# Layer 0's second MLP product half by seven quarter products, with the remainder dealt out under the first attention

## The chip, the cores and the metric

The kernel runs on one core of one Trainium2 chip. The metric is the device time of one launch in microseconds (us); lower is better. The engines are named as in the profile: PE is the matrix engine, PEld its weight load, DVE the vector engine, ACT the scalar engine, POOL the general engine, SP the engine that issues nearly all DMAs.

## What is computed

Two decoder layers on 1024 tokens of width 1024, in float32. Layer 0 mixes with a gated convolution of 31 taps and an attention on 256 memory rows; layer 1 with a three-branch sparse attention (compressed, selected, window) and a memory attention. Behind each mixing stand an output projection and an MLP:

```python
x = x + mix @ w_out[l]
x = x + squared_relu_mlp(rms_norm(x, norm_mlp_g[l]), w_mlp_in[l], w_mlp_out[l])

def squared_relu_mlp(h, w_in, w_out):          # w_in 1024 x 4096, w_out 4096 x 1024
    return jnp.square(jax.nn.relu(h @ w_in)) @ w_out
```

Layer 1's mixing reads `x` as it stands behind layer 0's MLP, so all of that MLP for a token's half must be done before the half's attention is prepared.

## The kernel before

**Halves and tiles.** The tokens are two halves of 512 (`hf` 0 and 1). Activations lie with the width on the partitions, as 8 tiles of 128x512 (`x[hf][o]`, `act[kt]`). Every float32 product is made of three matmuls: an operand is split into a high part (ACT copies it to the matmul type, L90 or L113) and a low part (the difference, L91 or L114, on DVE or POOL), and high-high, high-low and low-high are summed in a PSUM bank. `mm3` (L83 to L85) issues such triples. One 128x512 matmul is the unit in which work is counted below.

**Order of the work.** Half 0 goes through layer 0 first: mixing, output projection (`w_out`, L413 to L415, tile `ps_wo`), MLP. Under half 0's MLP run half 1's projections and its convolution (`conv`, L715), each of whose six channel tiles is released by a mark, a pair of instructions in half 0's MLP named by the list `MB`. Then come half 1's `w_out`, the preparation of half 0's attention (norm and projections; tiles `ps_kc`, `ps_tok`), and that attention with half 1's layer-0 MLP beside it; after that half 0's output projection of layer 1, the preparation of half 1's attention, and that attention with half 0's layer-1 MLP dealt out under it; last half 1's `w_out` and the remaining products of layer 1's MLP. The order on each engine is set when the program is built, by a list scheduler that fills an engine's gaps from what is ready, by priority of program order; `issue_after` bars an instruction from being placed ahead of another. A `Feed` deals a generator of steps out between the attention's transposes: at each mark it takes steps until the done share equals the share of the attention that has passed.

**Layer 0's MLP** is `mlp`. For each of 16 chunks of 256 hidden rows, `proj_in` makes two hidden tiles (48 matmuls into `ps_i`, L454 to L456; the ReLU times the norm's factor on DVE at L465, square on ACT at L466, split at L90 and L91 into `hid`) and `proj_out` adds their products to the eight `x` tiles (48 matmuls into `ps_mo`, the add on DVE at L479). 768 matmuls a half go into each of the two products. `HELD` = 2 chunks' `proj_out` of half 0 come behind half 1's `w_out`, with whose norm (`inv_rms`) they share the time. The sum of squares for the next norm is taken tile by tile behind the last chunk (`after0`); `norm_steps` then sums it over the partitions (`ps_n`, L154), takes the root on DVE (L99, L100) and spreads the factor (`ps_r`, L168); DVE multiplies it into `h` (L182).

**Layer 1's MLP** has its second product by seven products of quarters instead of eight (class `Seven`). A chunk's two hidden tiles by two halves of the tokens are one 2x2 matrix of blocks, its weights another. P1 and P2 are plain and use half 0 alone (`outs`; P1 is gathered in the tiles `p1`, and added to both halves on POOL by `add_p1`, L688). For the others `late` fetches half 0's hidden tiles from memory (`hd`), makes half 1's (`pairs`, `hidden`, L522 to L524 and L528), forms sums and differences (four on DVE, `te`, and four on POOL, `sv`, L653 to L660), splits them, and multiplies: the chain P6, P7, P4 and the chain P5, P3 each leave a running sum in one PSUM bank (L679), which after each product is added to other tiles of `x` (L681).

## Time and profile before

| | |
|---|---|
| three runs | 2396.56, 2399.91, 2400.14 us; median 2399.91 us |
| the profiled execution | 2395.2 us, of which the span of the profile is 2393.4 us |
| busy over the span | PE 2313.6 us, PEld 1963.5, DVE 1733.0, POOL 1394.2, ACT 1301.2 |
| mean granted clock of PE | 0.985 of full speed |
| DMA | 259.25 MB, on average 108 GB/s |

The profiled execution is 1.4 us below the fastest of the three runs and 4.7 us below their median. Stages in the profile, by the tiles that PE writes: up to 252 us layer 0's mixing; 252 to 303 half 0's `w_out`; 303 to 651 half 0's MLP with the convolution of half 1; 651 to 732 half 1's `w_out` and what was held back; 732 to 897 the preparation of attention 0; 897 to 1204 attention 0; 1204 to 1290 the rest of half 1's MLP; 1290 to 1461 half 0's `w_out` of layer 1 and the preparation of attention 1; 1461 to 1932 attention 1; 1932 to 2035 half 1's `w_out` and the entry into the quarter products; 2035 to 2393 these products. In a row of windows a busy time is followed by the number of instructions, PEclk is the granted clock, and the last two columns are the mean busy share of the DMA engines and GB/s.

### The profile page before, as it was taken

The numbers are of one execution on the slowest core, as the hardware profiler recorded it, in microseconds if no ns is written. First come the engines' busy times: TensorE is split into PE (matmuls) and PEld (weight loads), VectorE is DVE, ScalarE is ACT, GpSimd is POOL, SyncE is SP. The second block draws the span as 40 slices with busy tenths as digits, with TensorE's granted clock in tenths as the row PEclk, the third lists the DMA queues.
The fourth block names the chain that finished last, engine by engine and source line by source line (L and its number), as shares of the span: only waits on it lengthen the run. The fifth ranks groups of instructions, "written<-read, shape, count | busy, mean of one in ns | idle before, by whom it ended". The sixth has DMA issues, their size and how long they took to land.

```text
span 2393.4 us, 36549 instructions
## 1 busy us (share of the span) xinstructions
PE 2313.6 (97%) x11926; PEld 1963.5 (82%) x11926; DVE 1733.0 (72%) x3476; ACT 1301.2 (54%) x2974; POOL 1394.2 (58%) x1280
## 2 busy tenths in 40 slices
PE   6998899999999899999999999999999999999999
PEld 5887687888778798888887888788888877888887
DVE  7897577998646857677654865777778856777777
ACT  5575555333544446777644555777777743333332
POOL 5866544455653325756645224476676628878975
PEclk8999899999999999999999999899999999999999
DMA  5212433323343424222235543322222245332331
GB/s 190 83 55 80 153 102 99 101 99 97 116 151 104 150 85 127 83 90 79 82 118 173 151 137 105 125 72 76 92 80 78 81 143 193 119 107 93 110 97 58
DMA packets 161823, 259.25 MB, mean 108 GB/s; under 512 B 18145, under 2 KB 49505, under 8 KB 161121
## 3 DMA queue, kind: packets, MB, share of 16 engines
q1 hardware_dynamic: 161632, 256.91, 33.4%
q8 instruction: 95, 1.56, 0.3%
q14 instruction: 96, 0.78, 0.1%
HBM read 217.52 MB, written 28.84 MB: 103 GB/s over the span
## 4 chain that ended last, share of the span: by engine, by line
PE 84%; DVE 6%; DMA 3%; issue 3%; ACT 2%; POOL 1%; SPq 0%; ACTq 0%; POOLq 0%; DVEq 0%
PE ps_mo L679 9%; PE ps_mo L83 5%; PE ps_mo L84 5%; PE ps_mo L85 5%; PE ps_i L455 4%; PE ps_i L456 4%; PE ps_i L454 4%; PE ps_i L522 4%; PE ps_i L524 4%; PE ps_i L523 4%; PE ps_t L1269 4%; PE ps_s L1226 4%; PE ps_o L1287 2%; PE ps_wo L413 2%; PE ps_wo L414 2%
## 5 line engine op out<-in xcount | busy, mean ns | idle before, releaser
L114 POOL TENSOR_TENSOR hl<-raw,hl 128x512 fp32r<-128x512 f32 x504 | 665.0, 1330 | 569.4 <-ACT hl L113 529.2
L113 ACT ACTIVATE hl<-raw 128x512 fp32r<-128x512 f32 x552 | 344.0, 629 | 463.0 <-PE ps_i L456 121.5
L679 PE MATMUL ps_mo<-leaf,wl 128*128 128x512 f32 x960 | 225.9, 389 | 0.3 <-DVE leaf L91 0.3
L522 PE MATMUL ps_i<-act,hl 128*128 128x512 f32 x512 | 210.9, 412 | 4.8 <-DVE b L528 4.1
L83 PE MATMUL ps_mo<-hid,hl 128*128 128x512 f32 x512 | 205.5, 402 | 9.8 <-DVE a L465 4.4
L679 PEld LDWEIGHTS ps_mo<-leaf,wl 128*128 128x128 f32 x960 | 180.2, 188 | 38.0 <-DVE leaf L91 0.7
L454 PE MATMUL ps_i<-act,hl 128*128 128x512 f32 x512 | 200.9, 392 | 3.1 <-ACT r L433 3.1
L524 PE MATMUL ps_i<-act,hl 128*128 128x512 f32 x512 | 201.2, 393 | 0.4 <-POOL hl L114 0.4
L455 PE MATMUL ps_i<-act,hl 128*128 128x512 f32 x512 | 201.5, 394 | 0.0
L456 PE MATMUL ps_i<-act,hl 128*128 128x512 f32 x512 | 201.3, 393 | 0.0
L85 PE MATMUL ps_mo<-hid,hl 128*128 128x512 f32 x512 | 201.1, 393 | 0.0
L84 PE MATMUL ps_mo<-hid,hl 128*128 128x512 f32 x512 | 201.1, 393 | 0.0
L523 PE MATMUL ps_i<-act,hl 128*128 128x512 f32 x512 | 200.8, 392 | 0.0
L479 DVE TENSOR_TENSOR x<-x,ps_mo 128x512 f32<-128x512 f32 x256 | 173.5, 683 | 33.1 <-PE ps_mo L85 31.7
L1279 DVE TENSOR_TENSOR PT<-ps_t,PT 128x512 fp32r<-128x512 f32 (+1 forms) x220 | 147.8, 673 | 48.3 <-ACT PT L1275 46.1
L1255 POOL TENSOR_TENSOR prob<-prob,small 128x1024 f32<-128x1024 f32 (+3 forms) x120 | 181.9, 1532 | 0.0
L1275 ACT ACTIVATE PT<-ps_t 128x512 fp32r<-128x512 f32 (+1 forms) x256 | 143.8, 566 | 59.9 <-PE ps_t L1269 57.6
L1238 ACT ACTIVATE prob<-ps_s,small 128x512 f32<-128x512 f32 (+3 forms) x240 | 141.5, 591 | 61.3 <-DVE small L1236 48.3
L1226 PE MATMUL ps_s<-KS,Q 128*128 128x512 f32 (+5 forms) x552 | 144.5, 361 | 3.8 <-ACT prob L1238 3.8
L681 DVE TENSOR_TENSOR x<-x,ps_mo 128x512 f32<-128x512 f32 x160 | 106.5, 681 | 41.5 <-PE ps_mo L679 40.9
L715 DVE SCALAR_TENSOR_TENSOR ca<-vB,taps,ca 128x512 f32<-128x512 f32 x174 | 130.6, 751 | 2.1
L83 PEld LDWEIGHTS ps_mo<-hid,hl 128*128 128x128 f32 x512 | 96.7, 189 | 33.5 <-DVE x L479 7.8
(341 smaller groups left out, 6268.8 us busy)
## 6 DMA issues: line engine op xcount, KB each, us to landing
raw<-in_w_mlp_in_dram SPq DMA_DIRECT2D x256, 256.0 KB, 2.7
raw<-in_w_mlp_out_dram SPq DMA_DIRECT2D x160, 256.0 KB, 2.8
...
```

The costliest lines, as they stand in the source:

```text
L83: nc.tensor.matmul(ps, lhsT=lh, rhs=rh, start=(i == 0), stop=False)
L84: nc.tensor.matmul(ps, lhsT=lh, rhs=rl, start=False, stop=False)
L85: nc.tensor.matmul(ps, lhsT=ll, rhs=rh, start=False, stop=(i == n - 1))
L113: nc.scalar.activation(hl[:, 0, :n], raw[:, :n], AF.Copy)
L114: k.last_lo = k.lo_eng.tensor_tensor(hl[:, 1, :n], raw[:, :n], hl[:, 0, :n].bitcast(F32), op=ALU.subtract)
L454: nc.tensor.matmul(p_, lhsT=wh, rhs=h[kt][:, 0], start=kt == 0, stop=False)
L455: nc.tensor.matmul(p_, lhsT=wh, rhs=h[kt][:, 1], start=False, stop=False)
L456: nc.tensor.matmul(p_, lhsT=wl, rhs=h[kt][:, 0], start=False, stop=kt == KT - 1)
L522: nc.tensor.matmul(ps, lhsT=wh, rhs=h[kt][:, 0], start=kt == 0, stop=False)
L523: nc.tensor.matmul(ps, lhsT=wh, rhs=h[kt][:, 1], start=False, stop=False)
L524: nc.tensor.matmul(ps, lhsT=wl, rhs=h[kt][:, 0], start=False, stop=kt == KT - 1)
L679: nc.tensor.matmul(ps[i], lhsT=ws[y][:, u, m], rhs=bs[y][:, v], start=z + y + q == 0, stop=y == self.G - 1 and q == 2, skip_group_check=z > 0)
```

## The change

The plain `mlp` goes; layer 0 too is run by `Seven`, with chunks 0 to 7 plain (`whole`) and chunks 8 to 15 `cut`. Half 0 makes all its hidden tiles, the plain outputs, and of the cut chunks P1 and P2; `HELDM` = 96 of these matmuls stand behind half 1's `w_out`. Then `lates` runs half 1's hidden tiles of the cut chunks with P6, P7 and P4, on the PSUM banks `s` (three) and `ca`, and stores two weight sums and two hidden differences a chunk in memory (`sd`). P5 and P3 (`fifth`) read them back: together with half 1's plain chunks and with part of layer 1's output projection of half 0 (`w_part`, five of eight input tiles, whose sum goes through memory as `xq`) they are dealt out by a `Feed`, `AHEAD0` = 380 matmuls before attention 0's first transposes and the rest under it. Half 0's `w_out` of layer 1 keeps three input tiles, 72 matmuls instead of 192. The norm and first projections of attention 1 use the banks and pools of the work beside it (`km`), which lets them be placed under the end of attention 0. The low parts of weights in layer 0's `lates` go to DVE, POOL, POOL in turn (`Turns`).

```diff
+MIXORDP = (0, 1, 2, 6, 7, 3, 4, 5)
-MQB, HELD = 2, 2
+MQB = 2
 HOP, MEMHOP, AHEAD = 1, 3, 192
-MB = (1, 3, 4, 6, 8, 9)
+MB = (4,8,11,14,17,20)
+PLAIN, HELDM, AHEAD0, END0 = 8, 96, 380, 1.0
...
-def w_out(k, l, mix, x, resid, order):
+def w_out(k, l, mix, x, resid, order, runs=None):
...
+    runs = runs or (order[:4], order[4:])
...
-        for g, kts in ((order[0] // 4, order[:4]), (order[4] // 4, order[4:])):
-            w = [weights(k, k.i["w_out"][l, o + i][:, 512 * g:512 * g + 512], P) for i in range(WG)]
+        for kts in runs:
+            lo, n = min(kts), len(kts)
+            w = [weights(k, k.i["w_out"][l, o + i][:, P * lo:P * (lo + n)], P) for i in range(WG)]
...
+def w_part(k, l, mixd, leaf, runs, resid, dst):
...
+    for o in range(KT):
+        t = k.tmp.tile([P, HF], F32, tag="a", name="t", bufs=2)
+        nc.sync.dma_start(t, resid[:, o])
+        ps = k.psum.tile([P, HF], F32, tag=k.tag, name="ps_wo", bufs=k.nps)
+        for kts in runs:
+            w = weights(k, k.i["w_out"][l, o][:, P * kts[0]:P * (kts[-1] + 1)], P)
+            for kt in kts:
+                wh, wl = (w[kt - kts[0]][:, x] for x in range(2))
+                nc.tensor.matmul(ps, lhsT=wh, rhs=mix[kt][:, 0], start=kt == runs[0][0], stop=False)
+                nc.tensor.matmul(ps, lhsT=wh, rhs=mix[kt][:, 1], start=False, stop=False)
+                nc.tensor.matmul(ps, lhsT=wl, rhs=mix[kt][:, 0], start=False, stop=kt == runs[-1][-1])
+                if kt == runs[-1][-1]:
+                    nc.vector.tensor_add(t, t, ps)
+                    nc.sync.dma_start(dst[:, o], t)
+                yield 3
...
-def mlp(k, l, x, act, rms, after, order, held=0):
...
+class Turns:
+
+
+    def __init__(self, *engines):
+        self.engines, self.n = engines, 0
+
+    def tensor_tensor(self, *args, **kw):
+        self.n += 1
+        return self.engines[self.n % len(self.engines)].tensor_tensor(*args, **kw)
...
-    if not r:
+    if not r and lead:
...
+        if not (r or lead or g):
+            next(rms)
...
-            ps = [psum.tile([P, HF], F32, tag="mm", name="ps_mo", bufs=6) for _ in range(4)]
+            ps = [psum.tile([P, HF], F32, tag=t, name="ps_mo", bufs=n) for t, n in BANKS[self.l]]
...
+    def fifth(self, cs, kept):
+
+        k, nc, x = self.k, self.k.nc, self.x
+        ws, hs = ([], []), ([], [])
+        for z in range(2):
+            for c in cs:
+                ws[z].append(weight(k, kept(c)[z]))
+                raw = k.wpool.tile([P, 512], F32, tag="raw", name="raw", bufs=k.nraw)
+                nc.sync.dma_start(raw, kept(c)[2 + z])
+                hs[z].append(self.leaf())
+                split(nc, hs[z][-1][:, 0], hs[z][-1][:, 1], raw)
+        for two in ((0, 1), (2, 3)):
+            ps = [k.psum.tile([P, HF], F32, tag=k.tag, name="ps_mo", bufs=k.nps) for _ in two]
+            for z in range(2):
+                for i, p_ in zip(two, ps):
+                    m = slice(i * P, i * P + P)
+                    for y in range(self.G):
+                        w, h = ws[z][y], hs[z][y]
+                        for q, (u, v) in enumerate(((0, 0), (0, 1), (1, 0))):
+                            nc.tensor.matmul(p_, lhsT=w[:, u, m], rhs=h[:, v], start=z + y + q == 0,
+                                             stop=y == self.G - 1 and q == 2, skip_group_check=z > 0)
+                    o = (4, 0)[z] + i
+                    nc.vector.tensor_add(x[1][o], x[1][o], p_)
+                    k.pe(3 * self.G * HF / 2.4)
+                    yield 3 * self.G
+
+    def lates(self, pool, psum, groups, rms, chains, after, sizes, kept=None, sums=None):
...
             self.late(pool, psum, cs, cur, chains, after if last else None, sizes, kept)
-            if 0 < g < 5:
-                self.add_p1(g - 1)
+            for hf, i in (sums or PSUMS)[g]:
+                self.add_p1(i, hf)
             cur = nxt
 
+BANKS = ((('s', 3),) * 3 + (('ca', 1),), (('mm', 6),) * 4)
+PSUMS = [[]] + [[((0, 1), i)] for i in range(4)] + [[]] * 3
 CHAINS = (((6, 1, 0), (7, 1, 4), (4, 0, 4)), ((5, 1, 4), (3, 1, 0)))
...
-        with tc.tile_pool(name=f"na{hf}", bufs=1, side="right") as k.tmp:
-            k.start(norm_steps(k, h, x, [acc], None))
-            k.flush()
+        if hf:
+            km.start(norm_steps(km, h, x, [acc], None, k.lo_eng))
+            km.flush()
+        else:
+            with tc.tile_pool(name=f"na{hf}", bufs=1, side="right") as k.tmp:
+                k.start(norm_steps(k, h, x, [acc], None))
+                k.flush()
...
-        acc = []
-        rest0 = mlp(k, 0, x[0], act[0], r, after0(0, acc), MIXORD0, HELD)
-        marks = next(rest0)
+        more = pool(es, "hid2")
+        acc, acc1 = [], []
+        hd0, sd, hd = (dram.tile([16, n, P, HF], F32, name=nm) for n, nm in ((2, "hd0"), (4, "sd"), (2, "hd")))
+        groups = [(c, c + 1) for c in range(0, 16, 2)]
+        whole, cut = groups[:PLAIN // 2], groups[PLAIN // 2:]
+
+        def kept(c):
+            return [sd[c, j] for j in range(4)]
+
+        GORD = cut + whole
+        p1p = [ExitStack() for _ in range(2)]
+        p1 = [pool(p1p[i // 2], f"p1{i}").tile([P, HF], F32, name=f"p1{i}") for i in range(4)]
+        m0 = Seven(k, 0, x, act, (MIXORD0, MIXORD), p1, more, pslot[0], hd0, range(PLAIN, 16))
+        todo = Feed(k, m0.plain(GORD, 0, r), 0, 1)
+        todo.take(48 * 16 + 24 * PLAIN + 24 * 16 - HELDM)
         k.flush()
...
         for i in range(6):
-            with tc.issue_after(marks[MB[i]][0].ins), tc.issue_after(marks[MB[i]][1].ins):
+            with tc.issue_after(m0.marks[MB[i]][0].ins), tc.issue_after(m0.marks[MB[i]][1].ins):
                 conv(k, i, vB[i], taps, cvs[i], csum, None, NDVEB)
...
                 r = iter(list(w_out(kl, 0, act[1], x[1], ins["x"][1], MIXORD)))
-        list(rest0)
+        list(todo.steps)
+
+        def after(p, i):
+            if p in (6, 4):
+                after0(0, acc)({6: i, 4: 4 + i}[p])
+
+        with tc.tile_pool(name="st0", bufs=1, side="right") as st:
+            n = len(cut)
+            k.lo_eng = Turns(nc.vector, nc.gpsimd, nc.gpsimd)
+            m0.lates(st, k.psum, cut, r, CHAINS[:1], after, {"b1": 6, "wr": 8, "ws": 3, "bt": 3}, kept,
+                     [[]] + [[((0, 1)[:1 + i // 2], i) for i in range(4) if i * (n - 2) // 4 + 1 == g] for g in range(1, n)])
+            k.flush()
+        k.lo_eng = nc.gpsimd
         psA.close()
         k.psum = es.enter_context(psum_pool("ps2"))
         k.nps = 2
+        p1p[1].close()
 
...
-        attend(0, acc[0], lambda: None)
-        acc = []
-        list(mlp(k, 0, x[1], act[1], r, after0(1, acc), MIXORD))
+        act[0] = act_tiles(0)
+
+        def rest_of_h1():
+            for i, cs in enumerate(cut):
+                yield from m0.fifth(cs, kept)
+                if i in (1, 2):
+                    m0.add_p1(i - 1, (1,))
+            yield from m0.plain(whole, 1, None, after0(1, acc1))
+
+        xq = dram.tile([P, KT, HF], F32, name="xq")
+        n = 24 * len(cut) * 2 + 96 * PLAIN + 120
+        feed = []
+
+        def part():
+            assert feed[0].at > 8 * MEMHOP + 42 * HOP
+            yield from w_part(k, 1, mixd[0], m0.leaf, ((6, 7), (0, 1, 2)), xs[0], xq)
+
+        def between():
+            todo = (y for s in (rest_of_h1, part) for y in s())
+            feed.append(Feed(k, todo, n, (8 * MEMHOP + 84 * HOP) * END0))
+            feed[0].take(AHEAD0)
+            feed[0].total, feed[0].done = n - feed[0].done, 0
+            return feed[0]
+
+        attend(0, acc[0], between)
+        list(feed[0].steps)
         k.flush()
-        hd = dram.tile([16, 2, P, HF], F32, name="hd")
-        groups = [(c, c + 1) for c in range(0, 16, 2)]
-        m1 = Seven(k, 1, x, act, (MIXORD, MIXORD1), None, pool(es, "hid2"), pslot[0], hd, range(16))
+        p1p[0].close()
+        m1 = Seven(k, 1, x, act, (MIXORDP, MIXORD1), None, more, pslot[0], hd, range(16))
...
             act[0], x[0] = act_tiles(0), x_tiles(0)
-            load_mix(k, act[0], mixd[0], MIXORD, k.wpool, "raw", k.nraw)
-            rms0 = w_out(k, 1, act[0], x[0], xs[0], MIXORD)
+            load_mix(k, act[0], mixd[0], (3, 4, 5), k.wpool, "raw", k.nraw)
+            rms0 = w_out(k, 1, act[0], x[0], xq, MIXORDP, ((3, 4, 5),))
...
-        attend(1, acc[0], between)
+        attend(1, acc1[0], between)
```

By the built programs, 128x512 matmuls of the MLPs' second products are 2784 where they were 2880; those of the hidden tiles and output projections are as many as before.

DVE at the norm of attention 0 (`h` is the normed tile, `act` its low part or a tile of it, `x_5771` and the like an `x` tile of half 1), before:

```order
L182 TENSOR_TENSOR h<-ps_r,x_2552 128x512 x2
L465 SCALAR_TENSOR_TENSOR a<-ps_i,r 128x512
L91 TENSOR_TENSOR act_94<-h,act_94 128x512
L479 TENSOR_TENSOR x_5771<-x_5771,ps_mo 128x512
L91 TENSOR_TENSOR act_95<-h,act_95 128x512
L182 TENSOR_TENSOR h<-ps_r,x_2553 128x512
L91 TENSOR_TENSOR hid<-a,hid 128x512
L479 TENSOR_TENSOR x_5771<-x_5771,ps_mo 128x512
L182 TENSOR_TENSOR h<-ps_r,x_2553 128x512
L91 TENSOR_TENSOR act_96<-h,act_96 128x512
L479 TENSOR_TENSOR x_5772<-x_5772,ps_mo 128x512
L182 TENSOR_TENSOR h<-ps_r,x_2554 128x512
```

and after, where `leaf<-raw` is the low part of what `fifth` has read back, and L700 its add into `x`:

```order
L700 TENSOR_TENSOR x_5426<-x_5426,ps_mo 128x512
L184 TENSOR_TENSOR h<-ps_r,x_2552 128x512 x2
L700 TENSOR_TENSOR x_5426<-x_5426,ps_mo 128x512
L93 TENSOR_TENSOR act_7651<-h,act_7651 128x512
L700 TENSOR_TENSOR x_5427<-x_5427,ps_mo 128x512
L93 TENSOR_TENSOR act_7652<-h,act_7652 128x512
L184 TENSOR_TENSOR h<-ps_r,x_2553 128x512
L93 TENSOR_TENSOR leaf<-raw,leaf 128x512
L184 TENSOR_TENSOR h<-ps_r,x_2553 128x512
L700 TENSOR_TENSOR x_5427<-x_5427,ps_mo 128x512
L93 TENSOR_TENSOR act_7653<-h,act_7653 128x512
L93 TENSOR_TENSOR leaf<-raw,leaf 128x512
```

In place of half 1's first hidden tile and first plain outputs, DVE has the splits and adds of P5 and P3 between the steps of the norm.

PE at the norm of half 1 that precedes attention 1 (`ps_n` the sum over partitions, `ps_r` the spread factor, `ps_kc` and `ps_tok` the first projections), before:

```order
L415 MATMUL ps_wo<-act_14551,hl 128x512
L154 MATMUL ps_n<-ones,acc 128x1 x4
L415 MATMUL ps_wo<-act_14548,hl 128x512
L413 MATMUL ps_wo<-act_14549,hl 128x512
...
L414 MATMUL ps_wo<-act_14551,hl 128x512
L168 MATMUL ps_r<-ident,nr 128x128 x4
L413 MATMUL ps_wo<-act_14552,hl 128x512
...
L414 MATMUL ps_wo<-act_14551,hl 128x512
L415 MATMUL ps_wo<-act_14551,hl 128x512
L955 MATMUL ps_kc<-act_348,hl 128x512 x2
```

and after, where `ps_o` are the last products of attention 0:

```order
L449 MATMUL ps_wo<-leaf,hl 128x512
L450 MATMUL ps_wo<-leaf,hl 128x512
L156 MATMUL ps_n<-ones,acc 128x1 x4
L1303 MATMUL ps_o<-PT,V 128x256
L1306 MATMUL ps_o<-PT,V 128x256
L1303 MATMUL ps_o<-PT,V 128x256
L1306 MATMUL ps_o<-PT,V 128x256
L1303 MATMUL ps_o<-PT,Vc_2539 128x256
L170 MATMUL ps_r<-ident,nr 128x128 x4
L971 MATMUL ps_kc<-act_348,hl 128x512
L921 MATMUL ps_tok<-hl,act_348 128x292
L922 MATMUL ps_tok<-hl,act_348 128x292
```

The 33 matmuls of `w_out` between `ps_n` and `ps_r`, and the 25 between `ps_r` and the first projection, have become five matmuls of attention 0 and none.

More of the change, by code (lines that the diff above doesn't have):

```diff
@@ L424, in w_out @@
     return inv_rms(k, acc)
+def w_part(k, l, mixd, leaf, runs, resid, dst):
+    nc = k.nc
+    mix = {}
+    for kt in sum(runs, ()):
+        raw = k.wpool.tile([P, HF], F32, tag="raw", name="mix", bufs=k.nraw)
+        nc.sync.dma_start(raw, mixd[:, kt])
+        mix[kt] = leaf()
+        split(nc, mix[kt][:, 0], mix[kt][:, 1], raw)
+    for o in range(KT):
[13 more added lines that the diff above has]
+                yield 3
 def inv_rms(k, acc):
@@ L505, in take, with hidden @@
         while self.done < n:
-            self.done += next(self.steps)
-def hidden(k, l, c, j, act, order, r, rms, dst, done):
+            self.done += next(self.steps, float('inf'))
+def hidden(k, l, c, j, act, order, r, rms, dst, done, lead=True):
     nc = k.nc
     h = [act[kt] for kt in order]
-    if not r:
+    if not r and lead:
         next(rms)
@@ L629, in pairs @@
             for j in range(2):
-                list(hidden(k, self.l, c, j, self.act[1], self.orders[1], self.r[1], rms, lambda: t[:, j], lambda a: None))
+                list(hidden(k, self.l, c, j, self.act[1], self.orders[1], self.r[1], rms, lambda: t[:, j], lambda a: None,
+                            self.l == 1))
             out.append(t)
@@ L684, in late, with add_p1 @@
                 k.pe(12 * self.G * HF / 2.4)
-    def add_p1(self, i):
-        for hf, o in ((0, i), (0, i + 4), (1, i), (1, i + 4)):
+    def add_p1(self, i, halves=(0, 1)):
+        for hf, o in [(hf, o) for hf in halves for o in (i, i + 4)]:
             self.k.nc.gpsimd.tensor_tensor(self.x[hf][o], self.x[hf][o], self.p1[i], op=ALU.add)
-    def lates(self, pool, psum, groups, rms, chains, after, sizes, kept=None):
+    def fifth(self, cs, kept):
[23 more added lines that the diff above has]
+    def lates(self, pool, psum, groups, rms, chains, after, sizes, kept=None, sums=None):
         cur = self.pairs(groups[0], rms)
@@ L884, in conv_norm, with proj @@
         k.marks += [a, b] if n > 3 else []
-def proj(k, h, srcs, scol, n=256):
+def proj(k, h, srcs, scol, n=256, kw=None):
     nc = k.nc
@@ L896, in proj @@
         parts = src.shape[-1] // n
-        hl = weight(k, src, [k.cols[:, scol + kt + j:scol + kt + j + 1] for j in range(parts)])
+        hl = weight(kw or k, src, [k.cols[:, scol + kt + j:scol + kt + j + 1] for j in range(parts)])
         for c in range(4):
@@ L941, in by_pair, with kv_c @@
     return [mq[:, a].rearrange("p h (c d) -> p c h d", c=2) for a in range(2)]
-def kv_c(k, h):
+def kv_c(k, km, h, tag="mm"):
     nc = k.nc
-    pss = [k.psum.tile([P, HF], F32, tag="b", name="ps_kc", bufs=2) for _ in range(2)]
+    pss = [km.psum.tile([P, HF], F32, tag=tag, name="ps_kc", bufs=2) for _ in range(2)]
     for s in range(4):
         kt = 2 * s
-        w = weight(k, k.i["w_kvc"][s], [k.cols[:, C_KV + kt + j:C_KV + kt + j + 1] for j in range(2)])
+        w = weight(km, k.i["w_kvc"][s], [k.cols[:, C_KV + kt + j:C_KV + kt + j + 1] for j in range(2)])
         for which in range(2):
@@ L1326, in nsa, with attention @@
     values(*pend)
-def attention(k, hf, x, acc, act, slot, pslot, gate, KcS, Vc, hTA, tail, masks, mixd, kvd, Kd, Vd, between):
+def attention(k, km, hf, x, acc, act, slot, pslot, gate, KcS, Vc, hTA, tail, masks, mixd, kvd, Kd, Vd, between):
     nc, tc, ins = k.nc, k.tc, k.i
```

70 lines of the change are left out of this document (11 added, 59 removed).

## The prediction

> **What bounds the kernel now.** I read the page's busy times first, then the chain that ended last by engine, then the stages as windows, then PE's waits.
>
> ```profile
> span 2393.4 us, 36549 instructions
> PE 2313.6 (97%) x11926; PEld 1963.5 (82%) x11926; DVE 1733.0 (72%) x3476; ACT 1301.2 (54%) x2974; POOL 1394.2 (58%) x1280
> ...
> PE 84%; DVE 6%; DMA 3%; issue 3%; ACT 2%; POOL 1%; SPq 0%; ACTq 0%; POOLq 0%; DVEq 0%
> ```
>
> PE is busy for 97% of the span, and the chain runs through PE for 84% of it. So fewer matmuls shorten the kernel as long as the other engines keep up, and a wait of PE costs its own length. The stages say where there is room:
>
> ```profile
> core 0: us, PE busy (x) PEld busy (x) DVE busy (x) ACT busy (x) POOL busy (x), PEclk, DMA share, GB/s
> 303.00:651.00 348.00, 345.38 (x1572) 284.50 (x1571) 285.16 (x466) 157.71 (x302) 173.54 (x135) 1.00 0.31 100
> 651.00:732.00 81.00, 77.95 (x343) 63.18 (x343) 32.62 (x57) 36.67 (x63) 51.36 (x40) 1.00 0.47 151
> 732.00:897.00 165.00, 158.53 (x997) 142.11 (x996) 117.47 (x281) 77.55 (x162) 42.89 (x37) 0.98 0.37 113
> 897.00:1204.00 307.00, 307.00 (x1726) 266.64 (x1726) 224.63 (x642) 215.87 (x618) 185.66 (x209) 1.00 0.30 92
> 1204.00:1290.00 86.00, 83.17 (x364) 67.22 (x362) 43.86 (x65) 35.74 (x62) 40.95 (x32) 1.00 0.45 144
> 1290.00:1461.00 171.00, 162.81 (x1010) 146.20 (x1010) 112.35 (x274) 85.35 (x177) 58.70 (x48) 0.97 0.42 132
> 1932.00:2035.00 103.00, 96.75 (x418) 78.11 (x419) 61.32 (x76) 40.10 (x68) 64.05 (x44) 0.98 0.52 172
> 2035.00:2393.00 358.00, 354.66 (x1565) 293.42 (x1563) 270.24 (x315) 127.79 (x224) 279.76 (x190) 1.00 0.29 98
> ```
>
> In attention 0 (897 to 1204) PE is never idle; in the quarter products of layer 1 (2035 to 2393) it loses 3.3 of 358 us, though POOL is busy 78% and DVE 75% there. Time is lost where half of the tokens has to pass a norm: 6.5 us in the preparation of attention 0 (732 to 897), 8.2 in that of attention 1 (1290 to 1461), 6.25 at the entry into the quarter products (1932 to 2035), 3.05 behind layer 0's second `w_out` (651 to 732). These are the rows of waits that belong there (total, times, longest):
>
> ```profile
> PE ps_r L168 <- DVE nr L100: 5.4, 2, 3.2
> PE ps_mo L83 <- DVE a L465: 4.4, 1, 4.4
> PE ps_mo L83 <- DVE x L479: 4.1, 6, 1.4
> PE ps_i L522 <- DVE b L528: 4.1, 2, 3.6
> ...
> PE ps_wo L413 <- DVE x L417: 1.9, 1, 1.9
> ...
> PE ps_s L1158 <- DMA Q<-Q: 0.3, 1, 0.3
> ```
>
> Of all adds of the plain MLP into `x` only six made PE wait, 4.1 us together. The row of `ps_wo` is the longest wait between 1290 and 1461; the last is the one wait of PE for a DMA that the list shows.
>
> The price of a matmul, and of a wait:
>
> ```profile
> 2100.00:2200.00 100.00, 100.00 (x442) 82.81 (x442) 75.15 (x87) 36.61 (x64) 84.92 (x58) 1.00 0.33 107
> 800.00:830.00 30.00, 23.72 (x106) 18.41 (x105) 23.99 (x62) 14.42 (x31) 10.47 (x9) 0.89 0.39 129
> ```
>
> And in PE's timeline, the wait in brackets:
>
> ```profile
> 811.24 0.80 PE L83 MATMUL ps_mo<-hid,hl 128*128 128x512 f32 x1 [4.39 <-DVE a L465]
> 811.84 0.63 PE L84 MATMUL ps_mo<-hid,hl 128*128 128x512 f32 x1
> ```
>
> 442 matmuls of 512 columns in 100 us at full clock are 0.2262 us each. Behind the one wait of 4.39 us the matmuls start 0.6 and 0.42 us apart, and the granted clock of those 30 us is 0.89: 3.3 us are lost to the clock beside the wait, 7.7 together.
>
> **The change part by part.** The sum is made against the profiled execution, 2395.2 us.
>
> *(a) Fewer matmuls.* A chunk's second product costs 96 matmuls for both halves, by seven products 84. Eight chunks are cut: 8 x 12 = 96 matmuls less, x 0.2262 = -21.7 us. `w_part` and the smaller `w_out` are 120 + 72 = 192 matmuls, as before: nothing by number. Hidden tiles: as before.
>
> *(b) The entry into layer 0's quarter products.* Behind half 1's `w_out` the old kernel goes on to an attention's preparation with the held matmuls as cover (3.05 us lost); the new one goes to hidden tiles, as layer 1 does at 1932 to 2035 (6.25 us lost). The difference is +3.2; I take +3. Ends: -3.05, if all idle time of the stage goes, and +7.7, a whole wait with its clock loss.
>
> *(c) The flow of the quarter products.* The durations come from the same stage of layer 1:
>
> ```profile
> L681 DVE TENSOR_TENSOR x<-x,ps_mo 128x512 f32<-128x512 f32 x156 | 103.8, 681 | 40.8 <-PE ps_mo L679 40.2
> L91 POOL TENSOR_TENSOR wl<-wr,wl 128x512 fp32r<-128x512 f32 x59 | 86.3, 1476 | 27.5 <-ACT wl L90 27.5
> L91 DVE TENSOR_TENSOR leaf<-b,leaf 128x512 fp32r<-128x512 f32 x60 | 73.5, 1245 | 1.0 <-ACT leaf L90 1.0
> L114 POOL TENSOR_TENSOR hl<-raw,hl 128x512 fp32r<-128x512 f32 x43 | 60.0, 1409 | 8.7 <-ACT hl L113 8.7
> L660 POOL TENSOR_TENSOR wr<-wr 128x512 f32<-128x512 f32 x13 | 21.5, 1652 | 0.2
> L656 POOL TENSOR_TENSOR wr<-wr 128x512 f32<-128x512 f32 x13 | 19.2, 1475 | 0.2
> L688 POOL TENSOR_TENSOR x<-x,p 128x512 f32<-128x512 f32 x12 | 19.3, 1606 | 0.0
> L653 DVE TENSOR_TENSOR b<-b,b 128x512 f32<-128x512 f32 x12 | 18.2, 1514 | 19.9 <-ACT b L529 19.9
> L528 DVE SCALAR_TENSOR_TENSOR b<-ps_i,r 128x512 f32<-128x512 f32 x24 | 16.4, 684 | 15.2 <-PE ps_i L524 15.1
> L658 DVE TENSOR_TENSOR b<-b 128x512 f32<-128x512 f32 x12 | 14.7, 1228 | 0.0
> ```
>
> A group of two chunks is 96 matmuls of hidden tiles and 3 x 4 x 6 = 72 of P6, P7 and P4: 168 x 0.2262 = 38.0 us of PE. POOL: eight weight sums at 1.48 to 1.65, some 12.5 us; 8 low parts of weights, two in three on POOL, 5.3 x 1.409 = 7.5; six `wl` x 1.476 = 8.9; on average three adds of `p1` x 1.606 = 4.8; together 33.7, 89% of PE's time. DVE: four products with the norm x 0.684 = 2.7, eight differences at 1.23 to 1.51 = 10.6, six `leaf` x 1.245 = 7.5, twelve adds x 0.681 = 8.2, a third of the low parts, 2.7 x 0.80 = 2.1 (row below), together 31.1, 82%. Neither passes PE, and the old stage with P5 and P3 ran at 78 and 75% with 3.3 us lost in 358. So 0; ends 0 (a gain is excluded, the stage adds no room) and +6, if 89% loses as much in the four groups' 152 us as the worst stage above (8.2 in 171, so 7.3) instead of what the old stage did (3.3 in 358, so 1.4).
>
> The new DMAs, all on SP's queue (32 stores and 32 loads of `sd`, 16 and 16 of `hd0`, 8 and 8 of `xq`), I cost at nothing: they are asked for a group ahead, and PE's list of waits has a DMA for 0.3 us alone. Were that cover gone, a late load would hold the splits behind it.
>
> *(d) Preparation of attention 0.* P5 and P3 now run here, where half 1's first hidden tiles were:
>
> ```profile
> L479 DVE TENSOR_TENSOR x<-x,ps_mo 128x512 f32<-128x512 f32 x22 | 15.0, 680 | 4.7 <-PE ps_mo L85 4.5
> L114 DVE TENSOR_TENSOR hl<-raw,hl 128x512 fp32r<-128x512 f32 x16 | 12.6, 802 | 7.5 <-ACT hl L113 7.3
> L91 DVE TENSOR_TENSOR act<-h,act 128x512 fp32r<-128x512 f32 x8 | 6.7, 832 | 0.0
> L91 DVE TENSOR_TENSOR hid<-a,hid 128x512 fp32r<-128x512 f32 x7 | 6.2, 892 | 2.8 <-ACT hid L90 2.7
> L182 DVE TENSOR_TENSOR h<-ps_r,x 128x512 f32<-128x512 f32 x8 | 5.3, 677 | 2.9 <-PE ps_r L168 2.9
> ```
>
> By the built order DVE has here 29 adds of `ps_mo` where it had 22, and 14 `leaf` where it had 7 `hid`: 7 x 0.680 + 7 x 0.892 = 11.0 us, or 16 if the splits take 1.245 as above. On 117.5 busy of 165 that is 78 to 81%. Ends: all of it on PE's path, +16; all of the stage's idle time gone, -6.5, since P5 and P3 need nothing of the norm and can stand anywhere. I take a third of 11 to 16: +4, because the norm's steps queue on DVE in between, while elsewhere in the stage the projections give cover.
>
> *(e) End of attention 0 and preparation of attention 1.* Three pieces. First, 1204 to 1290, the MLP's rest behind attention 0, loses 2.8 us; its work now lies under the attention: -2.8. Second, between `ps_n` and `ps_r` of the norm PE has five matmuls instead of 33, and none instead of 25 behind it. The root on DVE (the longest wait for it was 3.2 us, with cover) now lies bare, then a first `h` at 0.677 and its high part on ACT:
>
> ```profile
> L90 ACT ACTIVATE act<-h 128x512 fp32r<-128x512 f32 x8 | 4.9, 629 | 5.8 <-DVE h L182 5.8
> ```
>
> That is 3.2 + 0.68 + 0.63 = +4.5, and with a clock loss behind it as above, +3.3: together +7.8. Third, cover: `w_out` and hidden tiles in this stage fall from 154 + 71 = 225 matmuls to 72 + 109 = 181, 44 x 0.2262 = 10 us. The sum of the first two is +5.0, which I take. Ends: -8.2, when all idle time of the stage goes, since the norm now starts under the attention; +15, when the lost cover comes on top in full.
>
> The Trainium skill, "TensorE: Matmul & The Clock Gate", section "HAM oscillation — how this bites in real kernels", puts the array at half rate after gaps of more than about 3.4 us. By that rule the bare 3.2 us would not trip it, and the sum would be some 3 us lower. The trace differs: from 1290 to 1461 the clock was 0.97 though no wait there passed 1.9 us, and so I keep the loss.
>
> *(f) Convolution under half 0's MLP.* Half 0's MLP has fewer matmuls before half 1's statistics. The convolution's last sum on POOL, and the matmul that uses it:
>
> ```profile
> 593.22 1.28 POOL L728 TENSOR_TENSOR csum<-csum,conv 128x512 f32<-128x512 f32 x1
> ```
>
> PE, the same place:
>
> ```profile
> 598.73 1.02 PE L852 MATMUL ps_mu<-csum,ones 128*128 128x512 f32 x2
> ```
>
> The sum ends at 594.5, 4.2 us ahead. By the built order the matmul comes 162 matmuls earlier, 36.7 us, and DVE has 52 adds fewer ahead of the convolution's end (44 instead of 96, x 0.68 = 35 us) and one hidden tile more (1.6). Short by 3, within the 4.2: 0; ends 0 and +3.
>
> Sum: -21.7 + 3 + 0 + 4 + 5 + 0 = -9.7, so 2385.5 for an execution like the profiled one. That lies 4.7 us below the median of three; a median of the changed kernel may lie like either, so I add half, 2.4, here and below: 2388.
>
> **The rivals.** *A: all covers hold.* (a) and the 2.8 of (e) alone: -24.5, so 2373. For it: attention 0 and the quarter stage lose almost nothing, and P5, P3 and `w_part` can stand anywhere. Against it: each stage that passes a norm loses 3 to 8 us today, and one more is added.
>
> *C: the clock.* The waits at (b) and (d) are each as the one at 811, 7.7 us instead of 3 and 4: +8.4, sum -1.3, 2396, no change that can be told. For it: the single wait that is so priced stands in the same stage, behind a hidden tile on DVE. Against it: hidden tiles need no such chain in (d) any more.
>
> *D: DVE bounds attention 0's preparation and attention.* A product tile of P5 or P3 takes 6 x 0.2262 = 1.36 us on PE, and there are two PSUM banks; the add has to come within the next tile. If each of the 32 adds is late by the mean of the six waits above, 4.1 / 6 = 0.68, that is +21.9: sum +12.2, 2410, slower. It decides from 0.45 us an add on. For it: more DVE work in a stage that is already full of short steps. Against it: the plain adds have the same six matmuls a tile and waited six times in 256.
>
> That the change does not do what it says is excluded by the count of the matmuls.
>
> **How the numbers follow.** A measurement of this kernel tells 0.2%, 4.8 us, from no change: the band is 2395.1 to 2404.7. Chances: A 0.26, the forecast 0.40, C 0.17, D 0.17. The forecast's own range is 2379 to 2396. Faster: A, 0.36 of the forecast, and 0.04 of C, which lies at the band's edge: 0.66. Same: the rest of both, 0.17. Slower: D, 0.17. The range reaches down to 2366, A with one more stage's idle time (6.5) gone, and up to 2410, D; about 0.08 of D, 0.06 of A and 0.05 elsewhere are left out.
>
> **What would show it.** (a) 11926 matmul records less by about 96, at 0.226 us each where PE is full. (b) the idle time of PE from half 1's `w_out` of layer 0 into the first hidden tiles, against 6.25. (c) PE's busy share in that stage, above 98%. (d) waits of `ps_mo` for an add of `x` in attention 0's preparation: their sum is 4 by the forecast, 22 by D. (e) a wait of `ps_r` of about 3 us and of `ps_kc` behind it of about 1.3, with a granted clock below 1 there. The prediction is wrong if `x` of half 1 comes so early that the norm at (e) passes under the attention, which gives A, or if the splits that are read back stand ahead of the norm's steps on DVE, which gives D.

## The result, and the profile after

The changed kernel takes 2432.1 us (median of four runs, 2429.7 to 2438.8) where the kernel before takes 2398.9 (2396.6 to 2400.1): the ratio is 1.0144, interval 1.0121 to 1.0167. It is slower by 33 us; 2388 was forecast, with 2410 as the upper end. The profiled execution is the slowest of the four, 2438.8 us with a span of 2437.0, so that the profiles differ by 43.6 us and the medians by 33. With the 21.7 us of matmuls saved, the profiles have 65 us of loss to account for and the medians 55.

The page of the changed kernel, busy times and the chain that ended last:

```profile
PE 2315.6 (95%) x11830; PEld 1958.8 (80%) x11830; DVE 1778.1 (73%) x3466; ACT 1305.5 (54%) x3002; POOL 1458.3 (60%) x1318
...
PE 74%; DVE 9%; DMA 5%; POOL 4%; issue 4%; ACT 3%; SPq 0%; POOLq 0%; ACTq 0%; DVEq 0%
```

The 96 matmul records are gone (11926 to 11830), and yet PE is busy 2 us longer: the mean granted clock fell from 0.985 to 0.975, which is worth some 24 us of the span. PE's idle time rose from 79.8 to 121.4 us. Together: -21.7 (matmuls) + 24 (clock) + 41.6 (idle) = +44. Of the chain that ended last PE has 74% instead of 84.

The stages as windows, cut at the same events as those of before:

```profile
core 0: us, PE busy (x) PEld busy (x) DVE busy (x) ACT busy (x) POOL busy (x), PEclk, DMA share, GB/s
304.00:621.00 317.00, 312.81 (x1412) 257.46 (x1411) 255.17 (x409) 149.42 (x290) 155.41 (x119) 0.99 0.36 111
621.00:687.00 66.00, 65.94 (x290) 53.23 (x289) 19.23 (x37) 26.39 (x44) 45.87 (x37) 1.00 0.55 181
687.00:861.00 174.00, 157.41 (x664) 125.28 (x662) 137.42 (x146) 64.16 (x114) 132.95 (x90) 0.96 0.53 173
861.00:1026.00 165.00, 157.77 (x997) 142.36 (x997) 123.25 (x292) 79.09 (x167) 51.11 (x42) 0.98 0.43 129
1026.00:1344.00 318.00, 304.39 (x1676) 260.97 (x1675) 212.67 (x619) 214.78 (x626) 186.10 (x213) 0.98 0.36 108
1344.00:1510.00 166.00, 149.47 (x915) 133.63 (x916) 116.98 (x276) 84.03 (x177) 50.87 (x41) 0.92 0.45 136
1976.00:2078.00 102.00, 96.01 (x415) 77.39 (x415) 60.88 (x74) 39.04 (x66) 63.35 (x43) 0.98 0.54 173
2078.00:2437.00 359.00, 355.29 (x1568) 293.94 (x1566) 271.52 (x315) 128.72 (x226) 280.10 (x191) 1.00 0.30 97
```

What a row is short of its length is PE's idle time. Attention 0 (1026 to 1344) has 13.6 us of it at a clock of 0.98, where before it had none at 1.00, though 50 matmul records fewer are in it. Between attention 0's end and attention 1 (1344 to 1510) it is 16.5 us at 0.92; the two rows of before (1204 to 1461) had 11.0 at 0.97 to 1.00, with 91 us more of length to spread them over. The new stage (687 to 861) has 16.6 us at 0.96. The preparation of attention 0 (861 to 1026) has 7.2 where it had 6.5, half 0's MLP 4.2 where it had 2.6. Layer 1's quarter products are as before.

PE's longest waits in these stages (total, times, longest):

```profile
PE ps_s L1242 <- ACT prob L1254: 9.5, 9, 2.2
PE ps_mo L697 <- DVE x L669: 6.8, 1, 6.8
...
PE ps_wo L417 <- DVE gelu L1000: 5.0, 1, 5.0
...
PE ps_mo L667 <- DVE x L669: 4.1, 4, 1.5
PE ps_mo L697 <- DVE x L700: 4.0, 1, 4.0
PE ps_i L509 <- DVE hl L475: 3.1, 1, 3.1
```

The first row holds both attentions. In attention 0 alone (1027 to 1344) it is

```profile
PE ps_s L1242 <- ACT prob L1254: 5.2, 5, 2.2
```

where before there was no wait at all (the 3.8 us in 4 of before, and 4.3 in 4 here, lie in attention 1). Here score matmuls wait for ACT inside the attention's own chain; that nothing else was ready to be put between is an inference, which the runs below bear out. `ps_mo L697`, the first matmul of P5, waits 6.8 us for the last add of the quarter stage. The wait of `ps_wo` for `gelu`, 5.0 us at 1406 to 1411, is the longest between 1344 and 1510 and lies in the midst of the shortened output projection.

### The profile page after: what moved, and what is told of

Its sections match the earlier page's. It is cut to its first block, busy times and chain, and to the rows that moved or that the text cites. A ratio compares the mean times of both kernels' runs of the same rounds, so it can differ in the third digit from the quotient of the medians.

```text
span 2437.0 us, 36584 instructions
## 1 busy us (share of the span) xinstructions
PE 2315.6 (95%) x11830; PEld 1958.8 (80%) x11830; DVE 1778.1 (73%) x3466; ACT 1305.5 (54%) x3002; POOL 1458.3 (60%) x1318
## 4 chain that ended last, share of the span: by engine, by line
PE 74%; DVE 9%; DMA 5%; POOL 4%; issue 4%; ACT 3%; SPq 0%; POOLq 0%; ACTq 0%; DVEq 0%
PE ps_mo L667 10%; PE ps_i L507 7%; PE ps_i L509 7%; PE ps_i L508 7%; PE ps_t L1285 4%; PE ps_s L1242 4%; PE ps_mo L87 3%; PE ps_mo L85 3%; PE ps_mo L86 3%; PE ps_o L1303 2%; PE ps_wo L417 2%; PE ps_wo L418 2%; PE ps_wo L419 2%; PE ps_o L1306 2%; PE ps_a L85 2%
## 5 line engine op out<-in xcount | busy, mean ns | idle before, releaser
L116 POOL TENSOR_TENSOR hl<-raw,hl 128x512 fp32r<-128x512 f32 (+2 forms) x448 | 587.0, 1320 | 491.2 <-ACT hl L115 424.9
L115 ACT ACTIVATE hl<-raw 128x512 fp32r<-128x512 f32 (+2 forms) x528 | 325.7, 623 | 437.2 <-PE ps_i L509 108.4
L667 PE MATMUL ps_mo<-leaf,wl 128*128 128x512 f32 x1248 | 296.0, 390 | 5.6 <-DVE x L669 4.1
L667 PEld LDWEIGHTS ps_mo<-leaf,wl 128*128 128x128 f32 x1248 | 233.3, 188 | 58.6 <-DVE x L669 6.9
L509 PEld LDWEIGHTS ps_i<-act,hl 128*128 128x128 f32 x1024 | 193.3, 189 | 46.6 <-DVE hl L475 3.6
L507 PEld LDWEIGHTS ps_i<-act,hl 128*128 128x128 f32 x1024 | 193.6, 189 | 40.8 <-DVE b L515 4.1
L508 PEld LDWEIGHTS ps_i<-act,hl 128*128 128x128 f32 x1024 | 194.0, 189 | 37.2 <-DVE act L427 2.4
L85 PE MATMUL ps_mo<-leaf,hl 128*128 128x512 f32 x448 | 182.8, 411 | 1.7 <-DVE a L515 0.9
L86 PE MATMUL ps_mo<-leaf,hl 128*128 128x512 f32 x448 | 177.0, 396 | 0.0
L87 PE MATMUL ps_mo<-leaf,hl 128*128 128x512 f32 x448 | 176.5, 398 | 0.0
L669 DVE TENSOR_TENSOR x<-x,ps_mo 128x512 f32<-128x512 f32 x208 | 137.2, 680 | 43.1 <-PE ps_mo L667 42.5
L93 POOL TENSOR_TENSOR wl<-wr,wl 128x512 fp32r<-128x512 f32 x88 | 131.9, 1513 | 29.8 <-ACT wl L92 29.8
L92 ACT ACTIVATE wl<-wr 128x512 fp32r<-128x512 f32 x88 | 55.0, 625 | 134.4 <-PE ps_mo L667 113.7
```

Source lines behind the costliest of these rows:

```text
L85: nc.tensor.matmul(ps, lhsT=lh, rhs=rh, start=(i == 0), stop=False)
L86: nc.tensor.matmul(ps, lhsT=lh, rhs=rl, start=False, stop=False)
L87: nc.tensor.matmul(ps, lhsT=ll, rhs=rh, start=False, stop=(i == n - 1))
L115: nc.scalar.activation(hl[:, 0, :n], raw[:, :n], AF.Copy)
L116: k.last_lo = k.lo_eng.tensor_tensor(hl[:, 1, :n], raw[:, :n], hl[:, 0, :n].bitcast(F32), op=ALU.subtract)
L507: nc.tensor.matmul(ps, lhsT=wh, rhs=h[kt][:, 0], start=kt == 0, stop=False)
```

## The experiments

Theory S says that the change uses up the work that covered PE: 576 matmuls of half 1's MLP (384 of hidden tiles, 192 of products) no longer stand between the preparation of attention 0 and attention 1, since they have moved ahead of it or are saved. Its rivals are D (the even dealing by marks starves the places without marks), K (the pools that attention 1's norm now shares hold other work back), Q (at the quarter stage's exit, DVE's queue holds the adds up), and the quarter stage itself. Each kernel was compared with runs of the kernel before on the same chip, which had medians of 2393 to 2397.

**The cover alone, in the kernel before.** Half 1's MLP of layer 0 is cut from 16 chunks to 10 and to 12. Both kernels leave out a part of the product and serve for the time alone:

```diff
-        list(mlp(k, 0, x[1], act[1], r, after0(1, acc), MIXORD))
+        list(mlp(k, 0, x[1], act[1], r, after0(1, acc), MIXORD, NC=10))
```

> The kernel before with 10 instead of 16 chunks in half 1's MLP of layer 0, everything else as it was: 576 matmuls of that MLP are left out, as many as the change has moved ahead of attention 0 or saved (384 of hidden tiles, 192 of products). This measures the cover alone, with no quarter products, no dealing and no shared pools in it. Theory S: 576 x 0.2262 = 130.3 us leave PE, but attention 0 then runs out of matmuls and its norm and group switches stand bare, so that the time falls by only 95 to 110: 2285 to 2302. If cover is not the matter: the whole 130 come off, 2263 to 2268.

> The same with 12 chunks: 384 matmuls (86.9 us) left out, about what stood between the end of attention 0 and layer 1's output projection (361). Theory S: attention 0 is still full, and only the norm behind it and the start of the output projection lose their cover: the time falls by 70 to 80, 2314 to 2325. If cover is not the matter: 2306 to 2311. If already this costs as much as the shorter one: above 2330.

Measured: 2292.0 and 2316.3 against 2397.1. Of 130.3 us of matmuls 105.1 came off, of 86.9 it was 80.8. So 576 matmuls less cost 25 us of lost cover with no other part of the change in the kernel; the first 384 cost 6, the next 192 cost 19 (the intervals are some 4 us either way). The windows of attention 0 and of what follows, with 10 chunks:

```profile
897.00:1170.00 273.00, 264.81 (x1503) 227.57 (x1502) 208.29 (x617) 198.24 (x589) 166.84 (x194) 0.99 0.30 89
1170.00:1336.00 166.00, 147.41 (x931) 133.14 (x929) 121.57 (x274) 86.74 (x181) 50.46 (x40) 0.92 0.46 146
```

and with 12:

```profile
900.00:1201.00 301.00, 301.00 (x1698) 261.42 (x1697) 224.24 (x642) 213.79 (x613) 185.83 (x208) 1.00 0.31 93
1201.00:1366.00 165.00, 146.87 (x929) 132.95 (x928) 121.66 (x274) 87.54 (x183) 53.13 (x42) 0.93 0.47 149
```

With 12 chunks attention 0 is full (301.00 of 301.00), and what is lost is lost behind it; with 10 it is itself idle for 8 us at a lower clock. The waits behind attention 0 with 12 chunks show the bare norm:

```profile
PE ps_r L168 <- DVE nr L100: 4.9, 1, 4.9
PE ps_kc L954 <- ACT act L90: 3.9, 1, 3.9
PE ps_n L154 <- POOL acc L144: 2.6, 1, 2.6
```

**Dealing undone.** Half 1's rest follows attention 0 in program order, and the output projection is whole:

```diff
-        attend(0, acc[0], between)
-        list(feed[0].steps)
+        attend(0, acc[0], lambda: None)
+        list(rest_of_h1())
...
-            rms0 = w_out(k, 1, act[0], x[0], xq, MIXORDP, ((3, 4, 5),))
+            rms0 = w_out(k, 1, act[0], x[0], xs[0], MIXORD)
```

> The changed kernel with the dealing undone: half 1's rest (P5, P3 and the plain chunks) follows attention 0 in program order and fills its gaps by the scheduler, as the MLP did before, and layer 1's output projection of half 0 is whole again (192 matmuls) ahead of attention 1. The quarter products stay. Theory S (too little is left to cover): 384 hidden and 288 quarter matmuls of half 1 have moved ahead of attention 0, so the 960 that remain run out under it however they are dealt; the end of attention 0 stands bare and the time stays at 2425 to 2435. Theory D (the even dealing by marks starves the places without marks): attention 0 loses about 16 us as before, the preparation of attention 1 about 18, only the quarter stage's 25 us stay: 2399 - 22 + 25 + 5, about 2405.

Measured: 2437.1, ratio 1.0175 (1.0159 to 1.0190), 2 us above S's range and 32 above D's value. D falls as the cause by itself: with the dealing and the split projection undone and the shared pools kept, the time is no better.

**Dealing without quarter products.** All 16 chunks plain, no quarter products in layer 0 (`PLAIN` = 16, `lates` left out); the split projection and the shared pools stay as changed:

> The changed kernel without quarter products in layer 0 (all 16 chunks plain); half 1's whole MLP (1536 matmuls) and the 120 of the output projection's part are dealt out, 380 ahead and 1276 under attention 0. Theory S: there is work enough, attention 0 loses as before, the preparation of attention 1 keeps its 15 us too much for want of cover: about 2410. Theory D: attention 0 loses some 20 us more than before as in the changed kernel, 2430 or above. If dealing alone is harmless: 2395 to 2400.

Measured: 2426.3, ratio 1.0129 (1.0114 to 1.0144), between the two expectations. The windows of attention 0 and behind it:

```profile
894.00:1321.00 427.00, 421.29 (x2211) 356.06 (x2210) 241.10 (x650) 253.24 (x685) 246.81 (x260) 1.00 0.32 103
1321.00:1495.00 174.00, 150.91 (x941) 134.56 (x940) 122.28 (x290) 87.72 (x185) 52.34 (x40) 0.93 0.45 144
```

Attention 0 with 1276 matmuls dealt into it has a clock of 1.00 and 5.7 us idle in 427. But all the work is now inside it, and the norm behind it stands bare:

```profile
PE ps_r L170 <- DVE nr L102: 11.6, 1, 11.6
```

11.6 us in one wait, and a clock of 0.93 over that stage. S had that place at 15 us; the rest of the 31 lies in attention 0 (some 10 more than before, by its length less its matmuls at full clock, half of it idle time) and behind half 1's `w_out`, and was not expected. So the dealing, the split projection and the shared pools together cost 31 us where no matmul is saved or moved ahead: the work is there, but none of it stands over the norm. That is the mechanism of D, at a place behind the attention. None of the three was run alone, and their loss does not simply come on top of that of the quarter products: e7 below undoes all three and wins 9.

**The output projection whole, dealing kept.**

> The changed kernel with layer 1's output projection of half 0 whole again (192 matmuls ahead of attention 1, none dealt under attention 0); quarter products and dealing stay. Theory S: the preparation of attention 1 has its cover back and loses 18 us instead of 33, attention 0 with 120 matmuls fewer under it is no faster: 2417 to 2425. Theory D: attention 0 is bound by its own chain, so that 27 us of matmuls put back behind it cost about what the cover saves: 2428 to 2440.

Measured: 2431.6, ratio 1.0154 (1.0137 to 1.0171): no difference to the changed kernel. S's range (2417 to 2425) was missed, and D's (2428 to 2440) met. The preparation of attention 1 did lose some 14 us less, but attention 1 some 7 more: the projection started at 1352 us, where it started at 1290 before the change. That led to the next run.

**Own pools.** e1 with the norm and first projections of attention 1 in pools and banks of their own (`if hf:` ahead of `km.start` off, `kv_c(k, k, h, 'b')` and `proj(..., k)` for both halves):

> The undealt kernel (e1) with the norm and first projections of attention 1 in pools and banks of their own again, as before the change. Theory K (shared pools hold layer 1's output projection of half 0 back: its tiles wait until the norm is through, so that it starts at 1361 instead of 1290 us and its own norm at 1485 falls bare into attention 1): the projection covers the norm again, attention 1 loses 39 us instead of 47 and the preparation a few less: 2422 to 2430. If the shared pools are harmless: 2434 to 2440.

Measured: 2423.1, ratio 1.0123 (1.0104 to 1.0142), 14 us below e1, 12 by the ratios: K holds. The projection starts at 1330 us, where e1 has 1361. What is left is nearly that of the shortened kernel before (attention 0 and what follows):

```profile
1021.00:1308.00 287.00, 277.33 (x1546) 237.13 (x1546) 198.43 (x594) 200.65 (x596) 170.87 (x197) 0.98 0.29 88
1308.00:1469.00 161.00, 145.31 (x927) 130.92 (x926) 123.60 (x273) 85.91 (x181) 51.31 (x40) 0.94 0.47 150
```

9.7 and 15.7 us idle, where 10 chunks of the old MLP gave 8.2 and 18.6.

**The quarter stage's exit.** In DVE's timeline of the changed kernel the four last adds of P4 (L669) stand among the low parts of attention 0's weights (L122), which come as their weights' DMA allows:

```profile
845.24 0.88 DVE L122 SCALAR_TENSOR_TENSOR hl<-raw,cols,hl 128x256 fp32r<-128x256 f32 x2 [1.74 <-ACT hl L121]
846.03 0.68 DVE L669 TENSOR_TENSOR x<-x,ps_mo 128x512 f32<-128x512 f32 x1
...
848.42 0.68 DVE L669 TENSOR_TENSOR x<-x,ps_mo 128x512 f32<-128x512 f32 x1
849.02 0.90 DVE L122 SCALAR_TENSOR_TENSOR hl<-raw,cols,hl 128x256 fp32r<-128x256 f32 x1
849.84 0.68 DVE L669 TENSOR_TENSOR x<-x,ps_mo 128x512 f32<-128x512 f32 x1
850.44 2.30 DVE L122 SCALAR_TENSOR_TENSOR hl<-raw,cols,hl 128x256 fp32r<-128x256 f32 x2
852.66 0.67 DVE L669 TENSOR_TENSOR x<-x,ps_mo 128x512 f32<-128x512 f32 x1
```

The last add starts at 852.66, 6 us after PE's last matmul at 846.55. By the chain that ended last, the DMA of these weights was issued when POOL was done with the low parts of the quarter stage's weight sums:

```profile
840.39 1.31 POOL wl L93
...
841.73 0.33 SPq L112
...
842.11 2.60 DMA raw<-in_w_kvc_dram
```

From 819.20 to 841.70 this chain lies on POOL, in adds of P1, weight sums and low parts. Whether less work on POOL there would take the wait away was not run. Two runs put L122 behind the last add (e5), or behind the norm's first step (g3); `k.bar` is the one or the other:

```diff
+            with k.tc.issue_after(k.bar.ins) if getattr(k, "bar", None) else nullcontext():
+                nc.vector.scalar_tensor_tensor(hl[:, 1, s], raw[:, s], g, hl[:, 0, s].bitcast(F32),
```

> The changed kernel with one order more on DVE: the low parts of the scaled weights of attention 0's projections stand behind the last add of layer 0's quarter products. Theory Q (these parts, which wait for their weights' DMA, hold the last adds up): the wait of 6.8 us of PE for that add becomes 2 to 3 us, the half clock behind it 3 to 7 us instead of 10: 2424 to 2428. If the adds themselves are late or the bank is waited for otherwise: the wait stays above 5 us, 2430 to 2434.

> The changed kernel with DVE's low parts of attention 0's scaled weights put behind the first DVE step of the norm, not only behind the last add as in e5, so that neither the adds nor the read-back operands of P5 and P3 stand behind weights that wait for a DMA. Theory Q: the two waits of e5 (1.9 and 5.9 us) become one of at most 3, and the half clock behind it 3 to 7 us: 2422 to 2427. If what is late there is the DMA of the read-back operands or the adds as such: a wait of 5 to 7 us stays, 2428 to 2434.

Measured: 2429.5 (1.0141, 1.0122 to 1.0160) and 2425.0 (1.0123, 1.0108 to 1.0138). PE's waits there, in e5 and then in g3:

```profile
PE ps_mo L698 <- DVE x L701: 5.9, 1, 5.9
PE ps_mo L698 <- DVE x L670: 1.9, 1, 1.9
```

```profile
PE ps_mo L699 <- DVE x L702: 3.2, 3, 1.4
PE ps_mo L699 <- DVE x L671: 2.0, 1, 2.0
PE ps_mo L699 <- DVE ps_n L100: 0.9, 1, 0.9
```

In e5 the wait only moved: six of the low parts (842.47 to 849.01 on DVE) now stood ahead of the split of P5's operands and of P5's first add, for which PE waited 5.9 us. In g3 it is cut into pieces of 2.0 us and less, and the half clock is gone that ran in the changed kernel from 849.2, inside the wait, to 859.4. From 687 to 861 PE is idle for 13.4 us instead of 16.6, and the 6.0 us of half clock behind the wait had cost 3.0: Q holds, for some 6 us (7 by the times, 5 by the ratios, whose intervals overlap).

**P5 and P3 of the last group in the stage.**

> The changed kernel with the last cut group's P5 and P3 (48 matmuls, 10.9 us) taken right behind its P4, in the same banks, instead of being dealt out (332 instead of 380 matmuls ahead of attention 0's transposes). Theory S (cover): these matmuls need no new bank and stand over the norm of half 0, so the wait of 6.8 us and most of the half clock behind it go: the stretch from half 1's output projection to the first projection of attention 0 loses some 17 us instead of 27, 2420 to 2425. If the exit waits for something else (the adds, a DMA): the wait only moves, 2428 to 2434.

Measured: 2446.2, ratio 1.0215 (1.0188 to 1.0241), slower than the changed kernel. The cover brought waits of its own:

```profile
PE ps_mo L667 <- POOL wl L93: 5.5, 1, 5.5
PE ps_n L156 <- DVE x L669: 3.1, 1, 3.1
```

**Low parts on POOL alone** (`Turns` off):

> The changed kernel with all low parts of the weights of layer 0's quarter stage on POOL instead of DVE, POOL, POOL in turn. If DVE's share of them delays the first hidden tiles (the wait of 3.1 us for such a part on DVE at the entry): that wait goes and the stage is 3 to 6 us shorter, 2426 to 2429. If POOL is then the bound (its work rises by 3 x 1.4 us a group of 38 us, to about all of the time): the stage is 5 to 15 us longer, 2437 to 2447.

Measured: 2435.5, ratio 1.0165 (1.0150 to 1.0180), between the two: the wait of 3.1 us goes, and waits of 2.9 us for an operand and 3.5 for an add come in its place.

**Fewer cut chunks, and all repairs at once.** f8 and f12 join e1, e7 and e6, with 8 and 4 chunks. In f12 P1 is added to half 0's tiles behind the stores and squares of the last group, which therefore lack it; the instructions are the same in number.

> All three together with 8 chunks cut: P5 and P3 of the last group in the stage, nothing dealt, own pools. By S and K together: 2432 - 10 (exit) - 8 (pools), 2412 to 2420, since attention 0 still runs out of matmuls near its end and loses some 45 us where it lost 16. If the supply is not the matter and only exit and pools were: below 2400.

> As f8 with 4 chunks cut instead of 8: 48 matmuls saved instead of 96 (-10.9 us), and 288 hidden and quarter matmuls more are left for the stretch from attention 0 to attention 1. By S: attention 0 loses 16 to 20 us again, the preparation of attention 1 about 20, the quarter stage some 12: 2393 to 2403, faster than f8 though it saves half. If the quarter stage itself, and not what is left to cover, costs: about as f8.

Measured: 2431.5 (1.0159, 1.0142 to 1.0176) and 2419.3 (1.0100, 1.0081 to 1.0119). f8 missed; it holds e6's wait of 5.5 us for `wl` again. f12 missed its 2393 to 2403 too: it is the faster of the two, as S says, but not by as much. It holds a wait of 13 us of its own, told below. Without e6, with g3's order:

> Quarter products for 4 chunks instead of 8, with everything else that the other runs found costly undone: nothing dealt, output projection whole, own pools for attention 1's norm, the scaled weights' low parts behind the norm's first step; P1 is added to the x tiles behind the first of the two groups. By the account of the runs so far: 2396 - 10.9 for 48 matmuls, + 6 for 288 matmuls less behind attention 0 (as in the kernel before with 12 chunks), + 10 to 16 for the quarter stage's two ends, + 0 to 5 in half 0's MLP: 2401 to 2412, not faster than before. If the stage costs by its number of groups and not by its ends: + 8 instead, 2392 to 2400.

> The same with 8 chunks, which is e7 with DVE's order of g3. If the terms add up: 6 us below e7's 2423, so 2413 to 2420. If they overlap (the wait moves into the preparation of attention 0 when nothing is dealt ahead): 2421 to 2426.

Measured: 2411.8 (1.0077, 1.0054 to 1.0099) and 2417.6 (1.0097, 1.0080 to 1.0114), both within the account, h1 at its upper edge. e7 and g3 add up. In h1 half 0's MLP, `w_out`, quarter stage and attention 0 are:

```profile
304.00:624.00 320.00, 313.69 (x1427) 257.68 (x1426) 251.22 (x401) 150.23 (x290) 160.28 (x124) 1.00 0.32 105
624.00:700.00 76.00, 75.46 (x333) 61.11 (x331) 25.03 (x41) 28.43 (x46) 46.11 (x37) 1.00 0.48 164
700.00:822.00 122.00, 103.92 (x431) 81.62 (x432) 89.92 (x110) 44.89 (x79) 92.47 (x63) 0.96 0.46 148
971.00:1299.00 328.00, 326.46 (x1807) 281.84 (x1805) 213.00 (x614) 220.41 (x628) 199.13 (x220) 1.00 0.30 94
```

Attention 0 is full again (1.5 us idle). The stage of two groups is idle for 18.1 us, as much as that of four (16.6): the loss does not go by the number of groups. Of the 16.6 us, 4.3 lie between 687 and 715 and 8.2 behind 815, so most of it at the stage's ends. No version of the change that was run beats the kernel before.

## Why the prediction was wrong

**(a)** was right: the matmuls of all stages, each at its full-clock time, are 21.7 us less.

**(e) failed most.** It was put at +5, and attention 0 itself at nothing: the working said "PE is never idle" there and counted cover only behind attention 0, where its third piece, 10 us of lost cover, was left out of the sum. It never asked what would still be ready under the attention when 384 hidden-tile and 192 product matmuls were no longer left for it. The third piece was counted too low besides: from 1290 to 1461 the profile before has 192 matmuls of `w_out` and 72 of hidden tiles, the one after 72 and 108 from 1344 to 1510, which is 84 less, 19 us, where the working had 44 and 10. Attention 0 and the preparation of attention 1 lost 34 us more than before, by the length of the stages less their matmuls at full clock. Of this some 24 are the lost cover, by the same count alike in g1, where nothing else was changed, and in e7. The other 10 are not there in e7, which undoes the dealing, the split projection and the shared pools (its time is 9 us lower, 5 by the ratios); how they divide among the three stays open, and a part can be the profiled execution itself, which lies 6.7 us above the median of its kernel. The gain of 2.8 us for the MLP's rest behind attention 0 had the wrong sign: those 86 us were cover for the norm and let the output projection start ahead of it, and 384 matmuls less there cost 6 us (g2).

**(b) and (c)** were put at +3 and 0. From half 1's `w_out` to the end of attention 0's preparation 22 us more were lost. The entry came out better than forecast: 4.4 us idle from 621 to 715, with a longest wait of 3.1, where 6.25 was put. At the exit, which the sum did not have, PE waited 6.8 us, and 6.0 us of half clock stood behind the wait; some 6 us of this loss are DVE's queue (g3). The step "asked for a group ahead" looked at the DMAs of the stage and not at what else is issued onto DVE's queue while the stage ends. POOL and DVE did not bound the flow up to 815, where 4.1 of 100 us are idle. But the term took POOL's adds of P1 at an average of three a group, and six of them stand between 819 and 837, on the chain that leads to the exit. The remaining waits are short (four of `ps_mo` for an add, 4.1 us, among them) and are not each explained.

**(d)** was put at +4: 0.7 us more of idle time came, and the clock was the same. The late adds of rival **D** in the prediction fell with it: the one wait for an add of P5 or P3 is 4.0 us, not 22. (With the 2.4 us that the forecast adds, that rival decides from 0.53 us an add on, not from 0.45.) The side that was given 0.17, slower, came out by another mechanism.

**(f)** was put at 0 to +3; half 0's MLP lost 5 us more (4.2 idle instead of 2.6, and two half-clock pieces of 3.4 us where there were none). Its cause was not tried. These three sums, 34, 22 and 5, are 61 of the profile's 65 us; some 3 more lie in attention 1.

The bare wait at the norm itself was forecast at 3.2 + 1.3 us with half clock behind it, and the waits there are

```profile
PE ps_r L170 <- DVE nr L102: 3.8, 1, 3.8
PE ps_kc L971 <- ACT act L92: 1.4, 1, 1.4
PE ps_kc L972 <- DVE act L93: 1.4, 1, 1.4
```

at a clock of 0.92 over the stage: right in kind. The rule weighed there (the Trainium skill, "TensorE: Matmul & The Clock Gate", section "HAM oscillation — how this bites in real kernels") is not told apart from the row by it, since the wait came out at 3.8 us, above its mark of about 3.4.
